# A hybrid recurrent and attention block: second norm written in place, row factors on VectorE, early matmuls that only occupy TensorE, one weight group finished feature by feature, and the modulation blocks laid out anew

## The chip, the cores and the metric

The kernel runs on one core of a Trainium2 chip. A core has a matrix engine (TensorE; PE in the profile, with PEld for its weight loads), a vector engine (VectorE; DVE), an engine for activation functions (ScalarE; ACT), a general engine (GpSimd; POOL) and a queue processor that issues most transfers (SyncE; SP). The metric is the device time of one execution in microseconds; lower is better.

## The reference

One layer on x of shape (512, 2048) in float32. A conditioning vector c gives six modulation vectors of 2048 values:

```
mod = silu(c) @ w_ada + b_ada
sh1, sc1, gt1, sh2, sc2, gt2 = split(mod, 6)
h = rms_norm(x, g_mix) * (1 + sc1) + sh1
xr, yr, q, k, v, f_logit = split(h @ w_in)
y_rec = scan(conv(xr), gates) * gelu(yr)          # 1024 features, 8 blocks of 128
y_att = softmax(norm(q) norm(k)^T + cum - cum^T, causal) v   # 8 heads of 128
mix = concat(rms_norm(y_rec, g_out_rec), rms_norm(y_att, g_out_att))
x = x + gt1 * (mix @ w_out)
h2 = rms_norm(x, g_ffn) * (1 + sc2) + sh2
gate, up = split(h2 @ w_up)                       # 5632 features each
x = x + gt2 * ((silu(gate) * up) @ w_down)
```

cum is the running sum over the tokens of log sigmoid(f_logit + b_f), one per head.

## The kernel before, in words

All large products are made in a split form: an operand is rounded to the fast float32 form (`hi`), what is left over is kept (`lo`), and hi·hi, hi·lo and lo·hi are added in PSUM. So each weight tile needs one ScalarE copy and one VectorE subtraction (`wsplit`, L220 to L225), and each pair of tiles three matmuls (`mm`, L228). Features lie on the 128 partitions and the 512 tokens along the row for most stages. A "k-tile" is 128 rows of the contraction; there are 16.

The stages in order, by the names that their PSUM tiles have in the profile:

- `cps`: the second half of c is spread over the partitions by two matmuls with one row each, and SiLU follows (L108 to L112). Then VectorE has silu(c) in all partitions, and each modulation value is a multiply-and-sum of a row of w_ada with it: one "ada block" is 128 such values, two instructions of 128x1024 (L148, or L158 in the early, unqueued form `ada_fast`).
- `w1p`: xr, 8 features' tiles over 16 k-tiles (L358 to L384). Each k-tile needs an ada block for sc1, the factor `A`, the split `hph`, `hpl` of x·A, and the split of the weights. The sum of squares `ssq_x` runs along.
- `rstd_x`: the row factor 1/rms of each token. `rstd_parts` (L281) has two halves: `sums` adds the squares over partitions with four tiny matmuls and calls `rms_rstd` (L273: mean plus eps, then a power of -0.5, all on GpSimd), and `spread` brings the four columns back to all partitions with four matmuls against the identity. For x both halves are called at once by `rstd_bcast` (L396).
- `yr0p`: the first four tiles of yr (`fm_group`, L420). At fixed k-tiles hooks call `sh1_block`: an ada block for sh1 and `make_h` (L401), which makes the normalised h of one k-tile out of x, `rstd_x` and sh1. Six more such blocks hang on the next group.
- `h0p` to `h7p`: q, k, v of one head each, tokens on partitions (`tm_group`, L259). While one group's matmuls run, the attention of the head before it and, from head 2 on, the recurrent blocks in pairs run from hooks at given k-tiles (ATT_STEPS, REC_STEPS). `forget` (L447) makes cum in two hooks, at steps 4 and 6 of the first group after head 0; `make_spn` (L604) makes softplus of the recurrent parameter, which depends on inputs only. In `attention`, `qk_t` transposes q and k and also makes the bias tiles `bt`; `score` adds them, takes the exponential and multiplies by the reciprocal of the row's sum (L555), `pt_` transposes, `pv` multiplies with v.
- `yr1p`: the other four tiles of yr, then GeLU and the product with the scan's output (L814 to L826).
- `wo0p` to `wo3p`: the output projection in four groups; the eight attention tiles come first in the contraction. `mix_sums` and `mix_rec` (L831, L835) hang on steps 1 and 4 of the first group; `mix_rec` makes the spread of both row factors and splits the eight recurrent tiles.
- `up0p`, `up1p`, then `uf4p` to `uf43p` with seven products in place of eight, then the down projection `dn4p` to `dn2p`. The operands T of the seven products are made by `make_t` (L973) out of `make_h2` (L961), at hooks of up0 and up1.

48 ada blocks (gt1, sh2, sc2) wait in a list. `ada1` takes one block from it, behind the last weight split that has been traced, and starts the load of the next; five or six hooks per group do this from head 2 on, and WO_ADA=5 per output group. What is left in the list when the last output group ends is done by `with_a2` (L851) ahead of the factor `a2`, with which `make_hr` (L858) makes the operands of up0.

The order of the instructions on each engine is made by a planner ahead of the run: it takes what is ready by its own estimate of durations, the earlier traced or higher in priority first (`high_priority` moves an instruction up), and `issue_after` puts an instruction behind a given one on its engine. Each engine then works strictly in that order. Tiles with one tag share a number of buffers; a load waits until its buffer is free. The tag `ada` has two buffers, which one block fills, the tag `whi` and `wlo` three each, and the PSUM tag `acc` four.

Of the kernel before, what the change touches and what calls it, by code (L numbers as in the profile page):

```python
# [66 lines left out]
def block_kernel(ctx, tc, xT, crow, adaT, vecs, bfr, w1, wyr, wqkv0, wqkv, wgate, wout, wup0, wups, wdn, outT):  # L67
# [33 lines left out]
    with tc.high_priority(offset=100000):  # L101
        cr = wp.tile([P, 2048], F32, tag="raw", name="cr", bufs=RAW)
        nc.sync.dma_start(out=cr[:1, 1024:2048], in_=crow[:, 1024:2048])
        nc.sync.dma_start(out=c_b[:, :1024], in_=crow[:, :1024].broadcast_to([P, 1024]))
        one = cp.tile([P, P], F32, name="ones")
        nc.vector.memset(one, 1.0)
        nc.scalar.activation(c_b[:, :1024], c_b[:, :1024], AF.Silu)
        for q in (2, 3):  # L108
# [2 lines left out]
            nc.tensor.matmul(pc, lhsT=one[:1, :], rhs=cr[:1, cs], start=True, stop=True)
# [161 lines left out]
    def rms_rstd(ssum, out, n, inv=None):  # L273
        nc.gpsimd.tensor_scalar(out=out, in0=ssum, scalar1=1.0 / n, scalar2=EPS, op0=ALU.mult, op1=ALU.add)
# [2 lines left out]
        nc.gpsimd.tensor_tensor(out, out, mhalf[:, :out.shape[-1]], ALU.pow)
        if inv is not None:
            nc.gpsimd.tensor_mul(inv, inv, out)

    def rstd_parts(ssq, n, name, inv=None, times=None, bank=None):  # L281
# [4 lines left out]
        def sums():  # L286
            if len(ssq.shape) == 3:
                nc.vector.tensor_reduce(out=tok, in_=ssq, axis=AX.X, op=ALU.add)
            else:
# [3 lines left out]
                nc.vector.tensor_copy(out=tok, in_=ps[:, :NT])  # L293
            rms_rstd(tok, tok, n, inv)
            if times is not None:
                nc.gpsimd.tensor_mul(tok, tok, times)
# [1032 lines left out]
```

## Time and profile before

| | |
|---|---|
| three runs | 2059.55, 2063.02, 2065.53 us; median 2063.02 |
| the profiled execution | 2058.99 us, of which the span of the trace is 2057.3 us |
| busy: PE, DVE, ACT, POOL | 2028.0, 1706.8, 945.7, 110.6 us |
| instructions | 32497 |
| mean granted clock of TensorE | 0.998 |

The page gives for each engine the busy time in the span. A line of a timeline is: start in us, duration in us, engine, line of the kernel, operation, output and inputs, shapes, how many were merged, and in brackets the idle time before it with what ended it. A line of the waits is: who waited, for whom, then total us, times, longest us. The recorded duration of one matmul is longer than its share, since matmuls overlap; the distance from start to start is its price.

### The profile page before, as it was taken

To read this page: it belongs to the slowest core of one execution; us is meant where nothing else is said; L and a number is where in the kernel's file an instruction comes from. 1 tells how busy PE (TensorE), PEld (TensorE's weight loads), DVE (VectorE), ACT (ScalarE), POOL (GpSimd) and SP (SyncE) were. 2 spreads that over 40 slices of the span, in tenths; PEclk is the share of its full clock that TensorE was granted. 3 is DMA by queue.
4 is the path that set the end of the run, shared out by engine and by line. 5 is a ranking of instruction groups with operands and counts; after the bars stand their busy time and mean duration, and the time that the engine had idled before them with its cause. 6 is when DMAs were issued, how large, how long until landed. Compare 5 with 4: busy or idle time off the path is not lost.

```text
span 2057.3 us, 32497 instructions
## 1 busy us (share of the span) xinstructions
PE 2028.0 (99%) x12505; PEld 1847.4 (90%) x12505; DVE 1706.8 (83%) x2549; ACT 945.7 (46%) x1321; POOL 110.6 (5%) x141
## 2 busy tenths in 40 slices
PE   8999999999999999999999999999999999999999
PEld 6889998888788888999999999999999978888887
DVE  8999769987887649988898889888898877777796
ACT  4433447765422446444444444444444444545443
POOL 0000111111100000001000000000000000000000
PEclk9999999999999999999999999999999999999999
DMA  9989866767778732348888879988888586676894
GB/s 345 339 287 319 283 216 220 237 210 247 253 273 314 271 133 100 123 136 226 255 232 230 244 226 256 263 235 228 240 240 224 167 279 240 238 250 240 280 327 167
DMA packets 175822, 493.36 MB, mean 240 GB/s; under 512 B 20625, under 2 KB 45105, under 8 KB 171570
## 3 DMA queue, kind: packets, MB, share of 16 engines
q1 hardware_dynamic: 156306, 437.79, 62.2%
q0 software_dynamic: 10144, 36.70, 9.4%
q10 hardware_dynamic: 9216, 16.78, 2.3%
q8 instruction: 98, 1.61, 0.3%
q14 instruction: 58, 0.48, 0.1%
HBM read 455.53 MB, written 93.35 MB: 267 GB/s over the span
## 4 chain that ended last, share of the span: by engine, by line
PE 89%; DVE 7%; DMA 2%; issue 1%; POOL 1%; ACT 0%; SPq 0%; DVEq 0%; POOLq 0%; ACTq 0%
PE w1p L228 4%; PE dn6p L228 3%; PE dn3p L228 3%; PE dn2p L228 3%; PE dn7p L228 3%; PE dn1p L228 3%; PE dn5p L228 3%; PE dn4p L228 2%; PE yr1p L228 2%; PE up0p L228 2%; PE wo2p L228 2%; PE wo3p L228 2%; PE wo1p L228 2%; PE up1p L228 2%; PE yr0p L228 2%; PE wo0p L228 2%
## 5 line engine op out<-in xcount | busy, mean ns | idle before, releaser
L148 DVE SCALAR_TENSOR_TENSOR ada<-ada,c_b 128x1024 f32<-128x1024 f32 x96 | 116.2, 1220 | 24.1 <-DMA ada<-in_adaT 24.0
L223 ACT ACTIVATE uq_0sh<-uq_0r 128x1024 fp32r<-128x1024 f32 x40 | 42.4, 1060 | 113.5 <-DVE uq_0r L1081 110.4
L224 DVE TENSOR_TENSOR uq_0tl<-uq_0r,uq_0th 128x1024 fp32r<-128x1024 f32 x40 | 49.0, 1225 | 37.4 <-ACT uq_0th L223 37.4
L223 ACT ACTIVATE uq_0ah<-uq_0r 128x1024 fp32r<-128x1024 f32 x40 | 42.4, 1060 | 69.1 <-PE uf39p L1103 1.8
L1020 POOL DMA_DIRECT2D s2d<-in_wdn x44 | 36.4, 828 | 673.8 <-DMA s2d<-in_wdn 660.4
L223 ACT ACTIVATE uq_1ah<-uq_1r 128x1024 fp32r<-128x1024 f32 x40 | 42.4, 1061 | 59.3 <-issue 26.6
L224 DVE TENSOR_TENSOR uq_0al<-uq_0r,uq_0ah 128x1024 fp32r<-128x1024 f32 x40 | 49.0, 1226 | 24.9 <-ACT uq_0ah L223 23.6
L224 DVE TENSOR_TENSOR uq_0sl<-uq_0r,uq_0sh 128x1024 fp32r<-128x1024 f32 x40 | 49.0, 1226 | 18.3 <-ACT uq_0sh L223 18.3
L1123 ACT ACTIVATE ug<-ug 128x512 f32<-128x512 f32 x40 | 25.3, 632 | 84.3 <-DVE ug L1120 84.3
L223 ACT ACTIVATE uq_0th<-uq_0r 128x1024 fp32r<-128x1024 f32 x40 | 42.4, 1060 | 43.9 <-PE uf6p L1103 1.2
L223 ACT ACTIVATE uq_1th<-uq_1r 128x1024 fp32r<-128x1024 f32 x40 | 42.4, 1061 | 32.8 <-PE uf43p L1103 1.1
L223 ACT ACTIVATE uq_1sh<-uq_1r 128x1024 fp32r<-128x1024 f32 x40 | 42.5, 1062 | 27.7 <-DVE uq_1r L1081 26.2
L228 PE MATMUL w1p<-hph,w1h 128*128 128x512 f32 x128 | 47.2, 399 | 5.7 <-ACT hph L370 5.7
L224 DVE TENSOR_TENSOR uq_1tl<-uq_1r,uq_1th 128x1024 fp32r<-128x1024 f32 x40 | 48.9, 1222 | 4.3 <-ACT uq_1th L223 3.2
L228 PE MATMUL w1p<-hpl,w1h 128*128 128x512 f32 x128 | 50.9, 398 | 0.1
L228 PE MATMUL w1p<-hph,w1l 128*128 128x512 f32 x128 | 50.8, 397 | 0.0
L224 DVE TENSOR_TENSOR uq_1sl<-uq_1r,uq_1sh 128x1024 fp32r<-128x1024 f32 x40 | 49.0, 1225 | 0.0
L1080 DVE TENSOR_TENSOR uq_0r<-uq_0r 128x1024 f32<-128x1024 f32 x40 | 48.8, 1219 | 0.0
L224 DVE TENSOR_TENSOR uq_1al<-uq_1r,uq_1ah 128x1024 fp32r<-128x1024 f32 x40 | 48.7, 1218 | 0.0
L1080 DVE TENSOR_TENSOR uq_1r<-uq_1r 128x1024 f32<-128x1024 f32 x40 | 48.7, 1217 | 0.0
L178 DVE SCALAR_TENSOR_TENSOR gt<-gt,c_b 128x512 f32<-128x512 f32 x64 | 43.8, 684 | 0.0
L158 DVE SCALAR_TENSOR_TENSOR ada<-ada,c_b 128x1024 f32<-128x1024 f32 x32 | 38.9, 1217 | 2.1 <-DMA ada<-in_adaT 2.1
(12769 smaller groups left out, 8123.2 us busy)
## 6 DMA issues: line engine op xcount, KB each, us to landing
ada<-in_adaT SPq DMA_DIRECT2D x128, 512.0 KB, 5.2
uq_1r<-in_wups SPq DMA_DIRECT2D x80, 512.0 KB, 8.0
uq_0r<-in_wups SPq DMA_DIRECT2D x80, 512.0 KB, 5.1
s2d<-in_wdn POOLq DMA_DIRECT2D x44, 512.0 KB, 9.0
adf<-in_adaT SPq DMA_DIRECT2D x32, 512.0 KB, 5.9
gt<-in_adaT ACTq DMA_DIRECT2D x64, 256.0 KB, 5.6
s2d<-in_wdn SPq DMA_DIRECT2D x22, 512.0 KB, 8.4
s4d<-in_wdn SPq DMA_DIRECT2D x22, 512.0 KB, 9.5
```

The lines of the kernel that those rows point to most:

```text
L148: nc.vector.scalar_tensor_tensor(out=t, in0=t, scalar=1.0, in1=cs, op0=ALU.mult, op1=ALU.mult, accum_out=ac)
L158: nc.vector.scalar_tensor_tensor(out=t, in0=t, scalar=1.0, in1=c_b[:, cs], op0=ALU.mult, op1=ALU.mult, accum_out=ada_acc[j][:, hf, i:i + 1])
L178: nc.vector.scalar_tensor_tensor(out=t, in0=t, scalar=1.0, in1=c_b[:, r * S:(r + 1) * S], op0=ALU.mult, op1=ALU.mult, accum_out=gt2_acc[:, ...
L223: tail_hi.append(nc.scalar.activation(R(hi[:, :n]), raw_ap, AF.Copy).ins)
L224: tail_lo.append(nc.vector.tensor_sub(R(lo[:, :n]), raw_ap, hi[:, :n]).ins)
L228: nc.tensor.matmul(ps, lhsT=R(l), rhs=R(r), start=start, stop=stop)
L1020: nc.gpsimd.dma_start(out=out[:, cs], in_=src[:, cs], accum_op=ALU.add)
L1080: nc.vector.tensor_add(blocks[:, 0:3:2], blocks[:, 0:2], blocks[:, 2:3].broadcast_to([P, 2, 512]))
L1123: nc.scalar.activation(g, g, AF.Silu)
```

## The change

- **Second norm in place.** `make_h2` writes into the tile `x1[kt]` itself. Before, it took one of two buffers.
- **Row factors.** In `rms_rstd` the mean plus eps and the products with the inverse move from GpSimd to VectorE, with raised priority; only the power stays on GpSimd. The mean is read from PSUM where it lies there. `rstd_bcast` goes; the spread of `rstd_x` becomes a hook of the first yr group at step 1, and the first two `sh1_block` hooks come at step 1.
- **The beginning.** The load of `vec` moves from SP's queue to ScalarE's, and `keep_on` adds matmuls whose result nobody reads: two of 128 columns ahead of the `cps` matmuls, eight behind them, and two of 512 columns with the first x tile. `make_spn` is put behind a weight split (`late=True`).
- **Forget sums.** `rest` is cut in two; three hooks at steps 1, 6 and 9. The bias tiles of `qk_t` become a step of their own, and head 0 gets its own list of steps.
- **Second yr group.** The last four k-tiles are taken feature by feature, and each feature's GeLU and product follow at once.
- **Output groups.** The ada hooks are at (11, 14), (0, 4, 8, 12), (0, 3, 6, 9, 12), (0, 3, 6, 9) in place of (0, 3, 6, 9, 12) in each. The spread for the attention's factor stays at step 4, the rest of `mix_rec` moves to step 5.

```diff
-FORGET_STEP = 4
+FORGET_STEPS = (1, 6, 9)
+RX_STEP = 1
-WO_ADA = 5
+WO_ADA = ((11, 14), (0, 4, 8, 12), (0, 3, 6, 9, 12), (0, 3, 6, 9))
+KEEP = (2, 8, 2)
...
+        nc.scalar.dma_start(out=vec, in_=vecs)
         one = cp.tile([P, P], F32, name="ones")
...
+        keep = acc("keep")
+        def keep_on(n, rhs):
+            for _ in range(n):
+                nc.tensor.matmul(keep[:, :rhs.shape[-1]], lhsT=one, rhs=rhs, start=True, stop=True)
+        keep_on(KEEP[0], one)
         for q in (2, 3):
...
-        nc.sync.dma_start(out=vec, in_=vecs)
+        with tc.issue_after(last.ins):
+            keep_on(KEEP[1], one)
...
+        held = []
         for n, (kt, hi, lo) in enumerate(stream(src, kts, width, name, **kw)):
+            if n >= len(kts) - by_feature:
+                held.append((n, kt, hi, lo))
+                continue
             for f in range(nf):
+                cell(n, f, kt, hi, lo)
...
+        for f in range(nf if held else 0):
+            for n, *w in held:
+                cell(n, f, *w)
+            if evac:
+                evac(f, ps[f])
+            for fn in hooks.get(held[f][0], ()) if hooks else ():
+                fn()
...
     def rms_rstd(ssum, out, n, inv=None):
-        nc.gpsimd.tensor_scalar(out=out, in0=ssum, scalar1=1.0 / n, scalar2=EPS, op0=ALU.mult, op1=ALU.add)
-        if inv is not None:
-            nc.gpsimd.tensor_copy(out=inv, in_=out)
-        nc.gpsimd.tensor_tensor(out, out, mhalf[:, :out.shape[-1]], ALU.pow)
-        if inv is not None:
-            nc.gpsimd.tensor_mul(inv, inv, out)
+        with tc.high_priority(offset=EVAC):
+            mean = out if inv is None else inv
+            nc.vector.tensor_scalar(out=mean, in0=ssum, scalar1=1.0 / n, scalar2=EPS, op0=ALU.mult, op1=ALU.add)
+            nc.gpsimd.tensor_tensor(out, mean, mhalf[:, :out.shape[-1]], ALU.pow)
+            if inv is not None:
+                nc.vector.tensor_mul(inv, inv, out)
...
+                if kt == 0:
+                    keep_on(KEEP[2], xt)
...
-    rstd_x = rstd_bcast(ssq_x, D, "rstd_x", bank=acc)
+    rx_sums, rx_spread = rstd_parts(ssq_x, D, "rstd_x", bank=acc)
+    rx_sums()
...
-    hk0 = {}
+    hk0 = {RX_STEP: [lambda: rx.append(rx_spread())]}
     for kt in range(10):
-        hk0.setdefault(kt * 8 // 5, []).append(lambda kt=kt: sh1_block(kt))
+        hk0.setdefault(max(RX_STEP, kt * 8 // 5), []).append(lambda kt=kt: sh1_block(kt))
...
-        log1p_exp(spn, zl, NB, "spn")
+        log1p_exp(spn, zl, NB, "spn", late=True)
...
-    yr1 = fm_group(wyr[1], list(range(KT)), hs_, "yr1", hooks=hk)
+    yr1 = fm_group(wyr[1], list(range(KT)), hs_, "yr1", hooks=hk, by_feature=4,
+                   evac=lambda f, p: rec_out(4 + f, gelu2(p, f"ge{4 + f}", "c")))
...
-        for n in range(WO_ADA):
-            add(hk, 16 * n // WO_ADA, ada1)
+        for n in WO_ADA[g]:
+            add(hk, n, ada1)
         if g == 0:
             add(hk, MIXREC_STEPS[0], mix_sums)
-            add(hk, MIXREC_STEPS[1], mix_rec)
+            add(hk, MIXREC_STEPS[1], lambda: st_att.append(att_spread()))
+            add(hk, MIXREC_STEPS[1] + 1, mix_rec)
...
-        t = ap_.tile([P, S], F32, tag="x", name=f"h2x{kt}", bufs=2)
-        nc.vector.scalar_tensor_tensor(out=t, in0=x1[kt], scalar=a2[:, kt:kt + 1], in1=r1[0], op0=ALU.mult, op1=ALU.mult)
+        t = x1[kt]
+        nc.vector.scalar_tensor_tensor(out=t, in0=t, scalar=a2[:, kt:kt + 1], in1=r1[0], op0=ALU.mult, op1=ALU.mult)
```

More of the change, by code (lines that the diff above doesn't have):

```diff
@@ L110, in block_kernel @@
             pc = acc(f"cps{q}")
-            nc.tensor.matmul(pc, lhsT=one[:1, :], rhs=cr[:1, cs], start=True, stop=True)
+            last = nc.tensor.matmul(pc, lhsT=one[:1, :], rhs=cr[:1, cs], start=True, stop=True)
             nc.scalar.activation(c_b[:, cs], pc, AF.Silu)
-        nc.sync.dma_start(out=vec, in_=vecs)
+        with tc.issue_after(last.ins):
+            keep_on(KEEP[1], one)
     ident = cp.tile([P, P], F32, name="ident")
@@ L292, in sums @@
                     nc.tensor.matmul(ps[:, t:t + 1], lhsT=ssq[:, t * P:(t + 1) * P], rhs=ones[:, 0:1], start=True, stop=True)
-                nc.vector.tensor_copy(out=tok, in_=ps[:, :NT])
-            rms_rstd(tok, tok, n, inv)
+            rms_rstd(tok if len(ssq.shape) == 3 else ps[:, :NT], tok, n, inv)
             if times is not None:
-                nc.gpsimd.tensor_mul(tok, tok, times)
+                with tc.high_priority(offset=EVAC):
+                    nc.vector.tensor_mul(tok, tok, times)
         def spread():
@@ L306, in rstd_parts @@
         return sums, spread
-    def rstd_bcast(*a, **kw):
-        sums, spread = rstd_parts(*a, **kw)
-        sums()
-        return spread()
     def square_acc(ssq, src, first, name, tag):
@@ L324, in log1p_exp @@
         q = small(w, name + "q", 2)
-        nc.scalar.activation(e, z, AF.Abs)
+        if late:
+            with tc.issue_after(tail_hi[-1]):
+                nc.scalar.activation(e, z, AF.Abs)
+        else:
+            nc.scalar.activation(e, z, AF.Abs)
         nc.scalar.activation(e, e, AF.Exp, scale=-1.0)
@@ L406, in make_h @@
         t = xs[kt]
-        nc.vector.scalar_tensor_tensor(out=t, in0=t, scalar=A[kt], in1=rstd_x, op0=ALU.mult, op1=ALU.mult)
+        nc.vector.scalar_tensor_tensor(out=t, in0=t, scalar=A[kt], in1=rx[0], op0=ALU.mult, op1=ALU.mult)
         h, l = page(f"hh{kt}", "h"), page(f"hl{kt}", "h")
@@ L523, in qk_t, with biases @@
             st["qk"] = qkT
+        def biases():
             if h == 0:
@@ L813, in block_kernel @@
         add(hk, MIX_STEPS[i], lambda i=i: mix_att(i))
-    yr1 = fm_group(wyr[1], list(range(KT)), hs_, "yr1", hooks=hk)
+    yr1 = fm_group(wyr[1], list(range(KT)), hs_, "yr1", hooks=hk, by_feature=4,
+                   evac=lambda f, p: rec_out(4 + f, gelu2(p, f"ge{4 + f}", "c")))
     for i in range(4, NH):
         mix_att(i)
-    gy = []
-    for f in range(4):
-        g, w = yr1[f], page(f"ge{4 + f}", "c")
-        nc.scalar.activation(w, yr1[f], AF.Square)
-        nc.vector.scalar_tensor_tensor(out=w, in0=w, scalar=1.0 / GELU_C, in1=g, op0=ALU.add, op1=ALU.mult)
-        nc.scalar.activation(w, w, AF.Tanh, scale=GELU_C * GELU_S)
-        nc.vector.scalar_tensor_tensor(out=w, in0=w, scalar=1.0, in1=g, op0=ALU.add, op1=ALU.mult)
-        gy.append(w)
-    for f in range(4):
-        rec_out(4 + f, gy[f])
     st_att = []
```

38 lines of the change are left out of this document (22 added, 16 removed).

## The prediction

> **What bounds the kernel now.** I read the busy shares first, then the list of what TensorE waited for, then the timelines around each of these waits. The page:
>
> ```profile
> span 2057.3 us, 32497 instructions
> PE 2028.0 (99%) x12505; PEld 1847.4 (90%) x12505; DVE 1706.8 (83%) x2549; ACT 945.7 (46%) x1321; POOL 110.6 (5%) x141
> ```
>
> TensorE idles for 2057.3 - 2028.0 = 29.3 us, so no change that leaves the matmuls alone can win much more than that. The waits of TensorE (total us, times, longest):
>
> ```profile
> PE pt L561 <- DVE bt L555: 6.7, 5, 2.3
> PE w1p L228 <- ACT hph L370: 5.7, 1, 5.7
> PE uf4p L1103 <- ACT uq_0ch L1077: 1.9, 1, 1.9
> PE rstd_xb L301 <- POOL rstd_xt L277: 1.8, 1, 1.8
> PE ratiob L301 <- POOL ratiot L296: 1.5, 1, 1.5
> PE pc L460 <- DVE lf L458: 1.4, 1, 1.4
> PE h0p L228 <- ACT hh L409: 0.9, 1, 0.9
> PE wo0p L228 <- ACT mx3h L216: 0.8, 1, 0.8
> ```
>
> Nearly every one of these lines is touched by the change. Each is a gap of a serial engine, so a closed gap moves all that follows, unless VectorE is full there and becomes the bound. That is the question at each step.
>
> **The beginning.** TensorE's timeline, the start and the first matmuls; then the price of a warm matmul from a long unbroken stretch of the chain; then the first matmul after w1p:
>
> ```profile
> 2.44 3.75 PE L111 MATMUL cps<-cr,ones 1*128 1x512 f32 x4 [2.44 <-DMA cr<-in_crow]
> 11.87 1.22 PE L228 MATMUL w1p<-hph,w1h 128*128 128x512 f32 x2 [5.69 <-ACT hph L370]
> 17.61 0.58 PE L228 MATMUL w1p<-hph,w1h 128*128 128x512 f32 x1
> 18.04 0.39 PE L228 MATMUL w1p<-hpl,w1h 128*128 128x512 f32 x1
> 1873.05 60.01 PE dn6p L228 x264
> 102.15 0.39 PE L228 MATMUL yr0p<-hph,yr_0h 128*128 128x512 f32 x1
> ```
>
> Up to 17.61 a matmul takes 0.43 us from start to start (18.04 - 17.61), and from there on 60.01/264 = 0.2273, as its shorter records (0.39 for 0.58) show too: the clock is at half until then. The second k-tile began at 102.15 - 15 x 24 x 0.2273 = 20.3. VectorE's timeline has the operands (`hpl` of the first, second and last k-tile) and one of the softplus instructions among them, and ScalarE's shows when x arrives:
>
> ```profile
> 12.30 0.16 DVE L333 SCALAR_TENSOR_TENSOR spn<-spn,spnq 128x8 f32<-128x8 f32 x1
> 12.38 0.74 DVE L371 SCALAR_TENSOR_TENSOR hpl<-x,A,hph 128x512 fp32r<-128x512 f32 x1
> 18.09 0.75 DVE L371 SCALAR_TENSOR_TENSOR hpl<-x,A,hph 128x512 fp32r<-128x512 f32 x1
> 94.11 0.74 DVE L371 SCALAR_TENSOR_TENSOR hpl<-x,A,hph 128x512 fp32r<-128x512 f32 x1
> 9.95 0.63 ACT L315 ACTIVATE ssq_x<-x 128x512 f32<-128x512 f32 x1 [1.34 <-DMA x<-in_xT]
> ```
>
> The second matmul waits for the first `hpl`, done at 13.1. The softplus chain (13 VectorE instructions of about 0.16, several of them between `A` and `hpl`) leaves this place, and `vec` leaves SP's queue ahead of the first ada load: I take 0.6 us for both, `hpl` at 12.5. If the clock is full by then, the k-tile ends at 12.5 + 23 x 0.2273 = 17.7 in place of 20.3: **-2.6**. VectorE permits it: the second `hpl` ends at 18.8, less about 1 us of softplus work, and the sixteenth at 94.9 against TensorE's need at 20.3 + 14 x 5.455 = 96.7 in the old timeline, about 2 us of room plus that 1 us. The cost of the added matmuls: two `cps` of 512 columns took 3.75, so one takes 1.9 and one of 128 columns 0.47. Eight of them fill 6.2 to 9.9 at the slow clock, with no real work ready. The two with x start at 9.95 and end at 11.9 warm or 13.7 cold; only the cold case delays anything, by 13.7 - 13.1 = 0.6. On ScalarE the issue of `vec` comes ahead of SiLU, which waits for c anyway; on VectorE the instructions that read `vec` stand ahead of the first ada block, so it must land before that one's load, as it did on SP's queue. Bounds: +0.6 to -2.9.
>
> The trace alone says only that 5.7 us of idling left the clock slow and that some 6 us of work raised it. [...]
>
> **The row factor of x, and a stretch where VectorE is full.** GpSimd's chain, VectorE's wait for it, VectorE's last operand for h0, and a window in between (busy of PE, PEld, DVE, ACT, POOL, then granted clock, DMA share, GB/s):
>
> ```profile
> 105.18 1.09 POOL L274 TENSOR_SCALAR rstd_xt<-rstd_xt 128x4 f32<-128x4 f32 x1 [103.55 <-DVE rstd_xt L293]
> 106.36 1.91 POOL L277 TENSOR_TENSOR rstd_xt<-rstd_xt,mhalf 128x4 f32<-128x4 f32 x1
> 110.15 0.75 DVE L407 SCALAR_TENSOR_TENSOR x<-x,A,rstd_x 128x512 f32<-128x512 f32 x1 [2.78 <-ACT rstd_x L304]
> 183.20 0.75 DVE L410 SCALAR_TENSOR_TENSOR hl<-x,sh,hh 128x512 fp32r<-128x512 f32 x1
> 140.00:160.00 20.00, 20.00 (x102) 18.33 (x101) 20.00 (x35) 6.17 (x8) 0.00 (x0) 1.00 0.99 337
> ```
>
> With the spread behind two k-tiles TensorE's wait of 1.8 goes: 24 matmuls (5.5) and the tiny sums after 102.15 put it at about 108.5, and the power, without the 1.09 ahead of it, is done near 107.2. But from 110 to 184 VectorE does not pause, and h0's last k-tile already waits 0.9 for it. On TensorE's side this stage could gain 2.6 + 1.8 + 0.9 = 5.3. On VectorE's side the chain starts again at the spread, which moves with the beginning (-2.6) and lies 0.2 later (108.5 against 108.3), plus what of the 2.78 idle the planner fills with ada blocks, now that it knows of a later spread. I take half, 1.4: -2.6 + 0.2 - 1.4 = **-3.8 for the beginning and this stage together**; bounds +0.8 and -5.3.
>
> **Forget sums.** The chain `lf` now has five k-tiles before its matmul (each 12 matmuls of 384 columns, 12 x 0.75 x 0.2273 = 2.0 us): **-1.4**, bounds 0 and -1.4. The 13 softplus instructions come into this place; VectorE fills it with bias sums that wait for nobody.
>
> **Row factors in the heads.** Head 3's factor, and the window behind it:
>
> ```profile
> 314.78 1.10 POOL L274 TENSOR_SCALAR ss<-ss 128x8 f32<-128x8 f32 x1 [25.23 <-DVE ss L504]
> 315.96 1.64 POOL L277 TENSOR_TENSOR ss<-ss,mhalf 128x8 f32<-128x8 f32 x1
> 317.63 0.69 DVE L511 TENSOR_TENSOR qk<-qk,ss 128x512 f32<-128x512 f32 x1 [1.80 <-POOL ss L277]
> 362.78 0.69 DVE L511 TENSOR_TENSOR qk<-qk,ss 128x512 f32<-128x512 f32 x1 [0.30 <-POOL ss L277]
> 409.07 0.69 DVE L511 TENSOR_TENSOR qk<-qk,ss 128x512 f32<-128x512 f32 x1 [1.80 <-POOL ss L277]
> 320.00:340.00 20.00, 20.00 (x115) 19.17 (x115) 20.00 (x39) 18.22 (x30) 2.68 (x4) 1.00 0.55 196
> ```
>
> In the heads with recurrent pairs VectorE is full from here to the late `bt`, so its wait for GpSimd reaches TensorE. 1.1 of the chain goes and one VectorE instruction of about 0.2 comes (as the 0.16 above): -0.9 in heads 3 and 5, -0.3 in head 4, where it waited only 0.30, and about half of 0.9 in the last head, whose `bt` is the last of the five waits: **-2.5**. Bounds 0 (the planner spends it on other work) and -6.7 (all five waits).
>
> **End of the second yr group.** The wait for `ratio` and the next one behind it are 1.5 + 0.8. GeLU began when the whole group was done:
>
> ```profile
> 542.04 1.87 DVE L821 SCALAR_TENSOR_TENSOR ge<-ge,yr1p 128x512 f32<-128x512 f32 x3
> 567.45 1.42 DVE L840 SCALAR_TENSOR_TENSOR hsr<-hsr,vec,ratio 128x512 f32<-128x512 f32 x2 [1.93 <-ACT ratio L304]
> ```
>
> By features the first PSUM tile is complete 36 matmuls, 8.2 us, sooner, the last at the old time; four chains that queued at 542 are spread over 534 to 548, and three ada blocks (2 x 1.22 each) leave the first output group. **-2.3**, bounds 0 and -2.3. The new product with the inverse on VectorE waits there for the power (1.9); behind it stand splits of wo0, each due in 5.5 us at the earliest, so I price it at 0. What the feature order can cost: two weight buffers of three are held to the end, so the next group's second split starts about 1.4 us before that end, and it is needed 5.5 us after it.
>
> **Ada blocks.** The new list holds 2 + 4 + 5 + 4 = 15 hooks. 31 blocks go into the heads and yr1, of 48: **two are left for `with_a2`**, ahead of `a2`. VectorE and TensorE:
>
> ```profile
> 693.71 2.08 DVE L862 SCALAR_TENSOR_TENSOR hrl<-x,a,hrh 128x512 fp32r<-128x512 f32 x3 [0.79 <-ACT hrh L861]
> 712.23 1.23 DVE L224 TENSOR_TENSOR wo_1l<-wo3r,wo_1h 128x1024 fp32r<-128x1024 f32 x1 [2.30 <-ACT wo_1h L223]
> 727.41 1.43 DVE L944 SCALAR_TENSOR_TENSOR x<-wo3p,mod,rstd_att 128x512 f32<-128x512 f32 x2 [3.08 <-PE wo3p L228]
> 729.25 0.39 PE L228 MATMUL up0p<-hrh,up_0h 128*128 128x512 f32 x1
> DMA to landing us min/median/max: 3.0/5.9/8.6
> ```
>
> `hrl` is traced behind the evacuation of L944 but ran 34 us ahead of it: the planner pulls forward what is ready. So the two blocks run right behind the last split of wo3: 713.5 to 715.9 the first; its buffers free the second load, 5.9 more, 721.8 to 724.2 the second, `a2` at 724.8, the first operands (0.7 + 0.75) at 726.3. TensorE asks at 729.25. **0**, with 3.0 us of slack; the slowest landing leaves 0.3. The operand work of about 8 us moves from 693 to 718 into the up0 group, whose k-tiles take 2.7 each.
>
> **Second norm in place.** uf4's wait of 1.9 is for the split `uq_0ch`, which stands on ScalarE's queue behind the last `h2x`:
>
> ```profile
> 823.82 0.72 ACT L964 ACTIVATE h2x<-h2x,mod 128x512 f32<-128x512 f32 x1 [1.59 <-DVE h2x L963]
> ```
>
> That `h2x` needed one of two buffers, held by the tile before it; in place it can be made earlier, and ScalarE's idle 1.59 goes: **-1.5**, bounds 0 and -1.9.
>
> **Sum.** -3.8 - 1.4 - 2.5 - 2.3 + 0 - 1.5 = -11.5. The profiled execution took 2058.99 (1.7 around its span), 4.0 below the median of 2063.02; so 2047.5 on its scale, and 2051.5 on that of the median.
>
> **The rivals.**
> - *VectorE swallows the first half.* The clock stays slow (-0.6 of the beginning remains, the spread's gap is given back at h0), and the heads' order spends the 2.5 elsewhere: -0.6 - 1.4 - 2.3 - 1.5 = -5.8, 2057.2. For it: the full windows above. Against: the 2.78 of idle.
> - *Everything closes.* -5.3 - 1.4 - 6.7 - 2.3 - 1.9 = -17.6, 2045.4. Against it: VectorE's full windows.
> - *Late `a2`, slower.* The planner puts the two blocks behind the evacuation at 727.4: 730 to 732.3, load 5.9, second block to 740.5, `a2` 741, operands 742.5. up0 starts 13 us late, and cold again (13 x 0.2 = 2.6): +15.6, 2067.1. It decides once `a2` is later than 727.8, and turns the sign past 740. Against it: the 34 us above.
> - *It does not do what it says.* The planner reorders everything and opens as many waits as it closes: 2063.
>
> **Chances.** Forecast 0.50, its own range 2047 to 2055; swallowed 0.25; everything 0.10; late `a2` 0.08; nothing 0.07. The 0.3% that a measurement of this kernel can tell is 6.2 us, so faster means below 2056.8: 0.50 + 0.10 + half of the swallowed case 0.12 = 0.72. Slower than 2069.2 is the tail of the late `a2`: 0.04. Same: 0.24. The range 2045 to 2061 leaves out the late `a2`, nothing, and the tail of the best case.
>
> **What would show it.** Right: matmuls 0.23 apart from the first k-tile on; no wait at `rstd_xb`, `pc`, `ratiob`; h0's wait at most about 2; waits for `bt` summing to about 4; up0 without a gap. Wrong: 0.43 apart past 12 us, a longer wait at h0p, a wait of up0p for `hrh`, or new waits of yr1p for its splits.

## The result, and the profile after

The changed kernel takes **2050.88 us** (median of six runs, 2049.28 to 2053.46) beside 2062.65 for the kernel before (six runs, 2059.55 to 2065.53): ratio **0.9944, 95% interval 0.9931 to 0.9957**. The forecast was 2051.5. Its profiled execution took 2049.87. One of the ten executions of a kernel below (before, with the second norm in place) took 2853.05 us at a mean granted clock of 0.655 and is left out of its ratio.

The page of the changed kernel, and what its TensorE waited for (total us, times, longest):

```profile
span 2048.2 us, 32491 instructions
...
PE 2030.6 (99%) x12529; PEld 1850.5 (90%) x12529; DVE 1707.4 (83%) x2560; ACT 944.7 (46%) x1321; POOL 98.1 (5%) x126
```
```profile
PE pt L597 <- DVE bt L591: 7.9, 5, 2.6
PE h0p L239 <- ACT hh L437: 1.4, 1, 1.4
...
PE h1p L239 <- DVE z L480: 0.7, 1, 0.7
...
PE po L609 <- ACT pT L601: 0.5, 1, 0.5
...
```

The rows for `w1p`, `rstd_xb`, `pc`, `ratiob`, `wo0p` and `uf4p`, each 0.8 to 5.7 before, are gone. The largest row, `bt`, is not smaller but larger: 7.9 for 6.7. The list alone does not say what each wait was worth; the times at which each stage's first matmul starts do. Shift is after minus before, step is what the stage ahead of it gave. The starts are rounded to 0.1 us, so a step, and what is reckoned from it, can be 0.1 off. For uf4p and uf5p it is the first matmul with `tb0h`, the thirteenth of the group, since in the kernel before two of uf5p's first ones stand among the last of uf4p:

| first matmul of | before | after | shift | step | step as forecast |
|---|---|---|---|---|---|
| yr0p | 102.2 | 99.2 | -3.0 | -3.0 (beginning) | -2.6 |
| h1p | 185.5 | 181.4 | -4.1 | -1.1 (row factor of x, less what h0 gave back) | -1.2 |
| h2p | 228.3 | 223.0 | -5.3 | -1.2 (forget sums) | -1.4 |
| h5p | 355.8 | 351.7 | -4.1 | +1.2 (nearly all of it in the group h2p) | |
| h6p | 400.5 | 399.6 | -0.9 | +3.2 (head 4) | |
| wo0p | 542.7 | 540.5 | -2.2 | -1.3 (most of it head 5) | -2.5 for the three rows of heads together |
| wo1p | 593.4 | 588.3 | -5.1 | -2.9 (ratio) | -2.3 |
| up0p, uf4p | 729.3, 822.3 | 724.2, 817.2 | -5.1 | 0 (ada blocks, a2) | 0 |
| uf5p | 846.6 | 837.4 | -9.2 | -4.1 (second norm) | -1.5 |

Behind uf5p nothing moves. Two steps are far from the forecast: the heads lose 3.1 where 2.5 were to be won, and the second norm in place brings 4.1 for 1.5.

The beginning in TensorE's timeline of the changed kernel:

```profile
2.27 3.78 PE L121 MATMUL cps<-cr,ones 1*128 1x512 f32 x4
5.98 3.78 PE L115 MATMUL keep<-ones 128*128 128x128 f32 x16
9.91 2.12 PE L115 MATMUL keep<-x,ones 128*128 128x512 f32 x4
11.82 1.19 PE L239 MATMUL w1p<-hph,w1h 128*128 128x512 f32 x4
12.86 0.39 PE L239 MATMUL w1p<-hpl,w1h 128*128 128x512 f32 x1
13.08 0.39 PE L239 MATMUL w1p<-hph,w1l 128*128 128x512 f32 x1
17.49 1.19 PE L239 MATMUL w1p<-hph,w1h 128*128 128x512 f32 x4
```

The eight added matmuls of 128 columns run slowly (0.47 each) up to 9.8. The two with x take 1.06 each, where a `cps` of the same width takes 1.89: the clock rises during the first of them (the first of the four records is 0.84 long, the others 0.59). From 12.86 on a matmul takes 0.22 to 0.23, and the second k-tile begins at 17.5 in place of 20.3.

For the second norm, these rows give the first matmuls with `tb0h` of two successive groups (name, count, durations in ns, first and last start). The kernel before comes first, with its wait behind these rows, then the kernel after:

```profile
L1103 PE MATMUL uf4p<-tb0h,uq_0ah x2: 283/283/283, 822.3 to 822.6; 128*128 128x256 f32 x2
L1103 PE MATMUL uf5p<-tb0h,uq_0ah x2: 283/283/283, 846.6 to 847.0; 128*128 128x256 f32 x2
...
825.78 0.39 PE L1103 MATMUL uf4p<-tc0h,uq_0ch 128*128 128x256 f32 x1 [1.91 <-ACT uq_0ch L1077]
827.35 0.41 PE L1103 MATMUL uf4p<-tc2h,uq_0ch 128*128 128x256 f32 x1
827.57 0.41 PE L1103 MATMUL uf4p<-tc2l,uq_0ch 128*128 128x256 f32 x1
```
```profile
L1131 PE MATMUL uf4p<-tb0h,uq_0ah x2: 283/283/283, 817.2 to 817.6; 128*128 128x256 f32 x2
L1131 PE MATMUL uf5p<-tb0h,uq_0ah x2: 283/283/283, 837.4 to 837.8; 128*128 128x256 f32 x2
```

From uf4p to uf5p it is 20.2 us after and 24.3 before. Of the 4.1 the row of the wait shows only 1.9; 1.5 more lie **behind** it, where 16 matmuls up to 830.3 are 0.21 apart in place of 0.12: the clock had fallen to half. The rest are gaps of 0.1 to 0.2 us in the timeline from 839 on.

The heads, at head 4. First the kernel before (GpSimd's mean and power, and VectorE's ada block beside them), then the changed kernel (ada block, mean, power, product with the factor):

```profile
360.83 0.20 POOL L274 TENSOR_SCALAR ss<-ss 128x8 f32<-128x8 f32 x1 [22.01 <-DVE ss L504]
361.11 1.64 POOL L277 TENSOR_TENSOR ss<-ss,mhalf 128x8 f32<-128x8 f32 x1
361.25 1.22 DVE L148 SCALAR_TENSOR_TENSOR ada<-ada,c_b 128x1024 f32<-128x1024 f32 x1 [0.51 <-DMA ada<-in_adaT]
```
```profile
357.19 1.21 DVE L159 SCALAR_TENSOR_TENSOR ada<-ada,c_b 128x1024 f32<-128x1024 f32 x1
358.33 0.17 DVE L301 TENSOR_SCALAR ss<-ss 128x8 f32<-128x8 f32 x1
358.57 1.64 POOL L302 TENSOR_TENSOR ss<-ss,mhalf 128x8 f32<-128x8 f32 x1 [23.86 <-DVE ss L301]
360.25 0.69 DVE L545 TENSOR_TENSOR qk<-qk,ss 128x512 f32<-128x512 f32 x1 [1.75 <-POOL ss L302]
```

GpSimd's mean had cost 1.10 in head 3 (in the prediction's rows) and costs 0.20 here, where the ada block came late from its transfer. After, the block stands between the reduction and the mean, and VectorE then idles for the whole power. From the reduction's start to the product it is 4.21 in heads 3, 5, 6 and 7 before and 4.25 after; in head 4 it is 3.31 before and 4.25 after.

### The profile page after: what moved, and what is told of

It reads as the page before. It is cut to its first block, busy times and chain, and to the rows that moved or that the text cites. A ratio compares the mean times of both kernels' runs of the same rounds, so it can differ in the third digit from the quotient of the medians.

```text
span 2048.2 us, 32491 instructions
## 1 busy us (share of the span) xinstructions
PE 2030.6 (99%) x12529; PEld 1850.5 (90%) x12529; DVE 1707.4 (83%) x2560; ACT 944.7 (46%) x1321; POOL 98.1 (5%) x126
## 4 chain that ended last, share of the span: by engine, by line
PE 90%; DVE 4%; issue 2%; DMA 2%; SPq 0%; ACT 0%; POOL 0%; DVEq 0%; ACTq 0%; POOLq 0%
PE w1p L239 4%; PE dn6p L239 3%; PE dn3p L239 3%; PE dn2p L239 3%; PE dn7p L239 3%; PE dn1p L239 3%; PE dn5p L239 3%; PE dn4p L239 2%; PE yr1p L239 2%; PE up0p L239 2%; PE yr0p L239 2%; PE wo2p L239 2%; PE wo3p L239 2%; PE wo1p L239 2%; PE up1p L239 2%
## 5 line engine op out<-in xcount | busy, mean ns | idle before, releaser
L239 PE MATMUL w1p<-hph,w1h 128*128 128x512 f32 x128 | 42.4, 391 | 0.0
```

The costliest lines, as they stand in the source:

```text
L239: nc.tensor.matmul(ps, lhsT=R(l), rhs=R(r), start=start, stop=stop)
```

## The experiments

Medians and ratios are against the kernel before, run on the same chip in turn with them; differences in stages come from the profiles.

| kernel | median us | ratio (95% interval) |
|---|---|---|
| the changed kernel, again | 2051.03 | 0.9948 (0.9932 to 0.9964) |
| heads' mean on GpSimd | 2053.52 | 0.9954 (0.9942 to 0.9967) |
| block right behind the mean | 2057.25 | 0.9981 (0.9971 to 0.9990) |
| block 0.4 us behind the mean | 2053.62 | 0.9957 (0.9942 to 0.9971) |
| without added matmuls | 2055.22 | 0.9966 (0.9956 to 0.9977) |
| second norm in a buffer | 2057.79 | 0.9976 (0.9965 to 0.9987) |
| before, second norm in place | 2058.69 | 0.9985 (0.9975 to 0.9995) |
| yr1 all together | 2055.93 | 0.9967 (0.9956 to 0.9979) |
| four blocks left | 2061.51 | 1.0003 (0.9990 to 1.0017) |
| head 0 on the common steps | 2049.20 | 0.9937 (0.9919 to 0.9954) |
| two blocks out of heads 3 to 5 | 2049.32 | 0.9933 (0.9920 to 0.9946) |
| one block out of heads 3 to 5 | 2044.18 | 0.9912 (0.9897 to 0.9926) |

**The same kernel again.**

> The kernel after, unchanged, beside the others on this chip: 2051. Its profile tells how far stage lengths differ between two executions of one program. If the order of instructions alone sets them, every stage is within 0.5 us of the first profile; if transfers set some, the heads' groups differ by 1 to 3 us, at waits that end with a transfer.

Stage starts agree within 0.3 us up to h2p and within 1.0 behind it. Two groups differ by more than the 0.5 that the first theory allowed: h3p takes 1.6 longer and h6p 1.4 less, and not at a wait for a transfer. The waits for `bt` in heads 3, 4 and 5 are 2.30, 2.61, 2.02 (2.30, 2.63, 1.87 in the first profile). So the order of instructions sets the waits, and what differs is mainly the clock: it is at half for 3.41 us from 270.6 and from 390.1 here, from 389.1 and from 436.9 in the first profile. From the down projection's first to its second phase this profile has 0.8 more. A single profile tells the start of a stage to about 1 us, and the length of one group to about 1.7.

**The added matmuls taken out.**

```diff
-KEEP = (2, 8, 2)
+KEEP = (0, 0, 0)
```

> The kernel after, without the twelve matmuls whose result nobody reads (the counts 2, 8, 2 set to zero); vec on ScalarE's queue and the late softplus stay. Theory: the clock of w1p's first k-tile is again at half, 0.43 us from matmul to matmul up to about 17.5 us: yr0p starts 2 us later than in the kernel after (99.2), and what VectorE gives back at h0p is less than half, so the time is 2052 to 2053. Rival (VectorE sets the pace through the first half and swallows it): yr0p 2 us later, h0p where it is, 2050.5 to 2051.5.

TensorE's timeline of this kernel:

```profile
12.06 0.79 PE L239 MATMUL w1p<-hph,w1h 128*128 128x512 f32 x1 [5.96 <-ACT hph L396]
...
13.87 0.63 PE L239 MATMUL w1p<-hph,w1h 128*128 128x512 f32 x1
14.29 0.63 PE L239 MATMUL w1p<-hpl,w1h 128*128 128x512 f32 x1
```

The matmuls are 0.42 apart again, up to 16.8. yr0p starts at 101.6 (+2.4), h0p and h1p 2.4 later too: all of it goes through VectorE's full stretch, and the rival that VectorE swallows it is wrong. So 2.4 of the beginning's 3.0 are the added matmuls. The other 0.6, as much as I had put on `vec` and the late softplus, is a remainder: no run takes these two out. The median lies 4.3 above the changed kernel's, more than either theory gave. A further 2.4 of the profile arise between h3p and h7p, where nothing was edited: three groups are 1.6 to 1.9 longer and one is 2.7 shorter. The stretches at half clock lie elsewhere, from 272.8, 347.9 and 440.1, three in place of two.

**The second norm, undone in the kernel after and done alone in the kernel before.**

```diff
-        t = x1[kt]
-        nc.vector.scalar_tensor_tensor(out=t, in0=t, scalar=a2[:, kt:kt + 1], ...)
+        t = ap_.tile([P, S], F32, tag="x", name=f"h2x{kt}", bufs=2)
+        nc.vector.scalar_tensor_tensor(out=t, in0=x1[kt], scalar=a2[:, kt:kt + 1], ...)
```

> The kernel after, with the second norm written into one of two buffers again, as in the kernel before. Theory: the wait of uf4p (1.9 us) is back, and TensorE runs at half clock for some 3.4 us behind it (matmuls of 256 columns 0.21 apart in place of 0.12), so uf4p takes 24 us again and the time is 2054 to 2055.5. Rival (the wait alone, as forecast; the other 2 us of this stage come from another part): 2052 to 2053.

> The kernel before with the second norm written in place, and nothing else of the change. Theory: this alone takes the wait of uf4p and the half clock behind it: uf4p to uf5p 20.2 us in place of 24.3, and the time 2058.5, 4.1 below the kernel before. Rival (the wait alone, as forecast): 1.5 to 1.9 below, 2061.

Undone, the wait of 1.9 is back, 16 slow matmuls behind it, and uf4p takes 24.4 again (+4.2 against the changed kernel). The median, 6.9 above the changed kernel's, lies above both ranges: in the profile 2.5 arise ahead of the edited stage and 1.2 in the down projection. Done alone in the kernel before (its rows):

```profile
L1103 PE MATMUL uf4p<-tb0h,uq_0ah x2: 283/283/283, 821.3 to 821.7; 128*128 128x256 f32 x2
L1103 PE MATMUL uf5p<-tb0h,uq_0ah x2: 283/283/283, 841.5 to 841.8; 128*128 128x256 f32 x2
```

Here it is 20.2, so -4.1 in this stage; the medians differ by 3.6. In this stage the one line of the change is worth about 4, needed and sufficient.

**The end of yr1 taken together again.**

```diff
-    yr1 = fm_group(wyr[1], list(range(KT)), hs_, "yr1", hooks=hk, by_feature=4, evac=...)
+    yr1 = fm_group(wyr[1], list(range(KT)), hs_, "yr1", hooks=hk)
+    for f in range(4):
+        rec_out(4 + f, gelu2(yr1[f], f"ge{4 + f}", "c"))
```

> The kernel after, with all 16 k-tiles of the second yr group taken together again; GeLU and the product follow for each feature when the whole group is done. Theory: TensorE waits for the ratio's spread again, about 1.5 us and 0.8 behind it, so from wo0p to wo1p it is 2.3 to 3 us longer than the kernel after's 47.8, and the time is 2053 to 2054. Rival (the gain of this stage came from the row factors on VectorE and from the ada blocks that left the first output group): wo0p to wo1p within 0.5 us of 47.8, 2051.

```profile
PE wo0p L239 <- ACT mx0h L227: 1.5, 1, 1.5
```

From wo0p to wo1p it is 51.0 for 47.8, +3.2. The wait's place is not the one I named: the ratio itself is early enough, the first recurrent tile `mx0h` is late, one step further down the same chain, and `mx0l` and `mx2l` behind it cost 0.5 and 0.4 more. The median, 2055.93, lies above both ranges. Of the 6.0 by which this profile lies behind the changed kernel's, 2.1 arise in the heads, ahead of the edit, with three stretches at half clock for two, and 0.9 in the down projection.

**More ada blocks left for the end.**

```diff
-WO_ADA = (..., (0, 3, 6, 9))
+WO_ADA = (..., (0, 5))
```

> The kernel after, with two ada blocks fewer in the last output group, so that four instead of two are left for the factor a2. Theory (the reckoning of the prediction's rival, with this kernel's rows): the blocks follow the last split of wo3 (708.3) one behind the other, 8 us each, since each waits for its buffers and its load: 708, 716, 724, 732, a2 at about 736.5, first operands at 738.5; up0p starts 14 us late, its first matmuls partly at half clock: 2065 to 2068. Rival (the planner finds another place for them, the blocks' loads come closer together): below 2058.

VectorE's row of the factor `a2`, in the changed kernel and here:

```profile
720.20 0.17 DVE L882 SCALAR_TENSOR_TENSOR a<-mod,vec 128x16 f32<-128x16 f32 x1
```
```profile
736.66 0.17 DVE L882 SCALAR_TENSOR_TENSOR a<-mod,vec 128x16 f32<-128x16 f32 x1
```

I had expected 736.5. up0p starts 13.4 later; 2.2 of this come back by up1p, and the median lies 10.6 above the changed kernel's, below the range of the theory (2065 to 2068) and above the rival's. So the mechanism of the slower rival is real; with two blocks left it does not reach TensorE.

**The heads: mean on GpSimd, block behind the mean, block 0.4 us behind it.**

```diff
+        if n == HEAD_DIM:
+            nc.gpsimd.tensor_scalar(out=out, in0=ssum, scalar1=1.0 / n, scalar2=EPS, ...)
+            nc.gpsimd.tensor_tensor(out, out, mhalf[:, :out.shape[-1]], ALU.pow)
+            return
```

> The kernel after, with the mean of the heads' row factors back on GpSimd (only for the eight heads; the three other factors keep it on VectorE). Theory: moving the mean bought nothing in the heads, because the planner's filler, an ada block of 1.2 us that used to lie beside GpSimd's mean, now stands on VectorE between the reduction and the mean, so VectorE still waits 1.75 us for the power. Undone, the stretch from h5p to h6p loses its extra 3.2 us (wait for bt 2.6 back to 1.4 and no half clock behind it), head 5's gain of 1.4 is lost: net 2048 to 2052, where the kernel after has 2050.9. Rival (the mean on VectorE is worth the forecast 2.5, and the 3.2 us come from elsewhere, the order of the bias tiles or of the steps): 2053 to 2054, and h5p to h6p as long as in the kernel after (47.9 us from first matmul to first matmul).

Head 4 of this kernel, VectorE and GpSimd:

```profile
362.56 1.21 DVE L159 SCALAR_TENSOR_TENSOR ada<-ada,c_b 128x1024 f32<-128x1024 f32 x1
362.73 1.10 POOL L300 TENSOR_SCALAR ss<-ss 128x8 f32<-128x8 f32 x1 [22.72 <-DVE ss L542]
363.91 1.64 POOL L301 TENSOR_TENSOR ss<-ss,mhalf 128x8 f32<-128x8 f32 x1
365.58 0.69 DVE L549 TENSOR_TENSOR qk<-qk,ss 128x512 f32<-128x512 f32 x1 [1.80 <-POOL ss L301]
```

The median is in the rival's range, but not for the rival's reason: from h3p to h7p this profile has 184.4 us for the changed kernel's 182.6, and the largest difference, 4.0 from h1p to h2p, is head 0's wait for `bt` (3.1 for 0.7) and 3.41 us at half clock behind it. VectorE's wait for a transfer of the bias sums there is 1.95 for 0.70. In heads 3 to 7 half of my theory stands: the mean's place is worth nothing, VectorE waits 1.80 for 1.75. The other half falls: with the mean on GpSimd head 4 does not get back the short wait of the kernel before (2.62 for `bt`). That one came from the block's late transfer, not from the mean. And in heads 2 to 7 the mean on GpSimd takes 1.10 whenever the block begins 0.2 us ahead of it, 0.20 when it does not: the 0.9 is a wait for VectorE, no work (in the rows above the mean ends at 363.83, the block's instruction at 363.77).

```diff
+    def ada_behind():
+        with tc.issue_after(means[-1]):
+            ada_some(1)
...
+            m = nc.vector.tensor_scalar(out=mean, in0=ssum, scalar1=1.0 / n, scalar2=EPS, op0=ALU.mult, op1=ALU.add)
+            if n == HEAD_DIM:
+                means.append(m.ins)
...
             for n in H_ADA:
-                add(hk, n, ada1)
+                add(hk, n, ada_behind if n == 4 else ada1)
```

> The kernel after, with the ada block of each group's fourth k-tile put behind the mean of the head's row factor on VectorE, so that the mean comes 1.2 us sooner and the block runs beside GpSimd's power. Nothing else is moved. Theory: VectorE's wait for the power falls from 1.75 to about 0.6 in heads 2 to 6, each wait for bt falls by up to 1.2 us (2.30, 2.63, 1.87 to 1.1, 1.4, 0.7), and the half clock behind the longest goes: 2044 to 2048. Rival (VectorE is full up to the last bt, and what the wait loses is only filled by other work that was due later anyway): 2050 to 2051.5.

Head 3 here, where the mean is at 310.87:

```profile
310.95 1.22 DVE L159 SCALAR_TENSOR_TENSOR ada<-ada,c_b 128x1024 f32<-128x1024 f32 x1
311.12 2.54 POOL L308 TENSOR_TENSOR ss<-ss,mhalf 128x8 f32<-128x8 f32 x1 [23.45 <-DVE ss L305]
313.69 1.29 DVE L551 TENSOR_TENSOR qk<-qk,ss 128x512 f32<-128x512 f32 x2 [1.52 <-POOL ss L308]
```

Neither range holds. In heads 3, 5, 6 and 7 the power takes 2.54 beside the block, the wait only goes from 1.75 to 1.52, and the kernel is slower by 6.4; the profile puts the loss into h3p to h7p (188.1 us for 182.6), at waits for `bt` of 2.5 and 0.8 + 2.0 and a new one of 1.7 for the copies of head 5's PSUM. Head 4 is different: there the block waits for its transfer and begins 0.65 behind the power, the power takes 1.64, the product starts 3.37 after the reduction, and the wait for `bt` is only 0.9.

```diff
+            if n == HEAD_DIM and pending:
+                with tc.issue_after(m.ins):
+                    m = nc.vector.tensor_reduce(out=idle, in_=c_b[:, :256], axis=AX.X, op=ALU.add)
+                means.append(m.ins)
...
+              with (tc.issue_after(filler[-1]) if h >= 2 else ExitStack()):
                 nc.vector.tensor_tensor(z, z, ss[:, 4 * a:4 * a + 4].unsqueeze(2).broadcast_to([P, NT, P]), ALU.mult)
...
-                add(hk, n, ada1)
+                add(hk, 2 if n == 4 else n, ada_behind if n == 4 else ada1)
```

> The kernel after; in heads 2 to 7 the mean of the row factor is followed on VectorE by a small reduction with one input (128x256, its result unused), then by the ada block that stood ahead of the mean, and the product with the factor comes behind that block. Theory from the runs so far: the power takes 1.64 us by itself and 2.54 when an ada block (two inputs from SBUF) begins on VectorE within 0.2 us of it, so a filler right behind the mean wins nothing; 0.4 us later it does not disturb the power. Then VectorE no longer idles 1.75 us in these heads, the waits for bt in heads 3, 4 and 5 fall from 2.3, 2.6 and 1.9 by 1.2 to 1.6 each, and the time falls to 2045 to 2048. Rival (the power is slowed by any work of VectorE beside it, or the product is now late by as much): power 2.5 or longer, and the time 2050 to 2057, as with the block right behind the mean.

Head 3: the power, the block, and VectorE 10 us later:

```profile
312.35 1.64 POOL L316 TENSOR_TENSOR ss<-ss,mhalf 128x8 f32<-128x8 f32 x1 [23.45 <-DVE ss L311]
312.50 1.22 DVE L161 SCALAR_TENSOR_TENSOR ada<-ada,c_b 128x1024 f32<-128x1024 f32 x1
...
321.08 1.22 DVE L161 SCALAR_TENSOR_TENSOR ada<-ada,c_b 128x1024 f32<-128x1024 f32 x1 [1.78 <-DMA ada<-in_adaT]
```

A block that begins 0.15 behind the power disturbs it no more, and is not held by it: the rival's reason is wrong, its range right. VectorE's idle at the power is closed, and the time does not fall: 1.78 idle appear where the next block waits for its transfer, and the waits for `bt` are 3.3, 1.3 and 0.9 + 2.0. The product, put behind the block, starts 4.60 after the reduction for 4.25, so this run closes VectorE's wait without shortening the chain. It shows that the idle time alone was not worth its price: in heads 3 and 5 the waits for `bt` grow, only in head 4 the wait falls, from 2.63 to 1.27.

**What does keep bt late: the blocks.** In the changed kernel, the end of head 4's chain, on VectorE, ScalarE and TensorE:

```profile
385.23 0.68 DVE L587 CUSTOM_DVE_ANT_0 bt<-s,bt 128x512 f32<-128x512 f32 x1
385.95 0.72 ACT L589 ACTIVATE bt<-bt,nm 128x512 f32<-128x512 f32 x1 [0.31 <-DVE nm L587]
386.44 1.21 DVE L159 SCALAR_TENSOR_TENSOR ada<-ada,c_b 128x1024 f32<-128x1024 f32 x1
387.59 0.15 DVE L590 RECIPROCAL sm<-sm 128x1 f32<-128x1 f32 x1
388.25 0.48 DVE L591 TENSOR_SCALAR bt<-bt,sm 128x512 f32<-128x512 f32 x1
388.78 0.85 PE L597 MATMUL pt<-ident,bt 128*128 128x128 f32 x4 [2.63 <-DVE bt L591]
```

The exponential and its row sum are done at 386.8, and the reciprocal stands behind an ada block of 1.2.

```diff
-            for n in H_ADA:
+            for n in (1, 4, 7) if 3 <= h < 6 else (1, 3, 6, 8, 11, 13) if h >= 6 else H_ADA:
-WO_ADA = ((11, 14), (0, 4, 8, 12), (0, 3, 6, 9, 12), (0, 3, 6, 9))
+WO_ADA = ((6, 8, 10, 12, 14), (0, 4, 8, 12), (0, 3, 6, 9, 12), (0, 3, 6, 9, 12))
```

> The kernel after, with two of the five ada blocks (those of k-tiles 10 and 13) taken out of the groups behind heads 3, 4 and 5 and laid into the two groups behind heads 6 and 7 (six blocks each), the first output group (five) and the last (five); two are still left for the end. Theory: the waits for bt in heads 3, 4 and 5 (2.3, 2.6 and 2.0 us, and 1.7 to 2 us of half clock behind one or two of them) are VectorE's backlog of ada blocks, 1.2 us each, between the mean and the last bt; three or four of them less there (after: 5 or 6 instructions, now 2) leave only the chain score, reduction, exponential, product: waits below 0.7 each, the time 2043 to 2047. Rival (the waits are that chain itself, since the planner's order leaves two k-tiles between the last score and the transposes): waits as long as before, the time 2050 to 2052, or more where the first output group waits for its ratio.

Heads 4 and 5 have no wait for `bt` left, head 3 one of 1.85; h7p starts 6.2 sooner than in the changed kernel. Then it is given back: 3.8 up to wo0p, 1.3 at wo0p, 1.3 at up0p. The median, 2049.32, lies in neither range. The largest loss, VectorE and TensorE at the start of yr1p:

```profile
487.74 1.23 DVE L159 SCALAR_TENSOR_TENSOR ada<-ada,c_b 128x1024 f32<-128x1024 f32 x1 [1.81 <-DMA ada<-in_adaT]
...
488.89 0.42 DVE L524 COPY qk<-h7p 128x256 f32<-128x256 f32 x1
...
489.68 0.50 PE L239 MATMUL yr1p<-hh,yr_0h 128*128 128x512 f32 x1 [1.73 <-ACT v L527]
```

A moved block waits 1.81 for its transfer, in order ahead of a copy that empties h7p's PSUM; ScalarE's copies wait for VectorE's (up to 2.7), TensorE for ScalarE's (1.73).

**Head 0's own list of steps.**

```diff
-        for n, f in zip((FIRST_STEPS if h == 0 else ATT_STEPS if h < NH - 1 else LAST_STEPS)[1:], att[1:]):
+        for n, f in zip((ATT_STEPS if h < NH - 1 else LAST_STEPS)[1:], att[1:]):
```

> The kernel after, with head 0 on the same list of steps as the other heads (its own list had been put in by the change). Theory: the waits of 0.7 for bt and 0.5 for pT in head 0's group come from the later steps of its own list; with the common one they go or shrink by about 1 us, but the bias tiles' place comes ahead of the running sums' transpose and TensorE may wait for cum there: 2050 to 2052, not to be told from no change. Rival (the own list is what keeps the forget sums off the path): a wait of 1 us or more for cum or bt in that group, 2052 to 2054.

The small waits in this group go, h3p starts 1.3 and 0.7 sooner than in the two profiles of the changed kernel. The medians are 2049.20 and 2051.03 and their intervals overlap, so the two are not told apart.

**One block out of heads 3 to 5.**

```diff
-            for n in H_ADA:
+            for n in (1, 4, 7, 10) if 3 <= h < 6 else (1, 4, 6, 8, 10, 13) if h == 2 else H_ADA:
...
-        for n, f in zip((FIRST_STEPS if h == 0 else ATT_STEPS if h < NH - 1 else LAST_STEPS)[1:], att[1:]):
+        for n, f in zip((ATT_STEPS if h < NH - 1 else LAST_STEPS)[1:], att[1:]):
...
-WO_ADA = ((11, 14), (0, 4, 8, 12), (0, 3, 6, 9, 12), (0, 3, 6, 9))
+WO_ADA = ((8, 11, 14), (0, 3, 6, 9, 12), (0, 3, 6, 9, 12), (0, 3, 6, 9))
```

> The kernel after, with head 0 on the common list of steps, and one ada block (that of k-tile 13) taken out of the groups behind heads 3, 4 and 5; one goes into the group behind head 2 (six blocks), where VectorE idles 3.6 to 6.8 us, one into the first output group (8, 11, 14), one into the second (0, 3, 6, 9, 12); the groups behind heads 6 and 7 and the last output group stay as in the kernel after, since there the moved blocks stood ahead of the evacuation of h7p and gave back 2.9 us, and 1.3 each at wo0p and up0p. Theory (blocks on VectorE set the waits for bt): h4p to h7p 2 to 4 us shorter than the kernel after's 140.2, nothing given back behind it, 1 us for head 0: 2045 to 2048. Rival (each block costs the same wherever it is put): 2049 to 2051.

```profile
span 2042.8 us, 32502 instructions
...
PE pt L597 <- DVE bt L591: 3.6, 4, 2.1
```

h4p to h7p takes 134.8 for 140.2, one stretch at half clock for two, nothing is given back ahead of the down projection, and the time is **2044.18, ratio 0.9912 (0.9897 to 0.9926)** to the kernel before: below the changed kernel's interval, and a little below the expected range. This interval overlaps that of head 0's list alone, whose edit this run contains; that edit lies ahead of h4p. VectorE still waits 1.63 to 1.75 for the power in heads 3 to 7. So with that wait left as it is, fewer blocks make `bt` come sooner.

## Why the prediction was right, and where it was not

The total was right, and two of its terms were not.

- **Beginning and row factor of x**, -3.8: measured -4.1. The split holds too (2.4 clock for 2.0, 0.6 the rest), and the added float32 matmuls do raise the clock, between 9.9 and 10.6. That it would be full by 12.5 was an assumption of mine that no run showed ahead of the change; with the added matmuls those of w1p are 0.22 to 0.23 apart from 12.86 on, without them 0.42 up to 16.8. No run undoes the row factor of x alone. h0 took back 0.9 of the 5.0 that had been won at h0p (waits of 1.4 and 0.7 there, 0.9 and 0.2 before).
- **Forget sums**, -1.4: measured -1.2, as a stage only; no run undoes them alone.
- **Row factors in the heads**, -2.5: measured +3.1 from h2p to wo0p. This is the step that failed, in two places. First, I read GpSimd's 1.10 as the price of a mean. The timeline of the kernel before had a row of 0.20 for head 4; the 1.10 are 0.20 of work and 0.9 of waiting for the ada block on VectorE (in head 3 that instruction ends at 315.82, the mean at 315.88). Moved, the block stands ahead of the mean instead, and the chain is as long as before (4.25 for 4.21). Second, I reckoned that VectorE's wait reaches TensorE through `bt` in every head. Closing that wait by the 0.4 us spacer did not shorten the waits for `bt` in heads 3 and 5; taking blocks away did. In head 4 the chain does count: where it is 3.3 to 3.4 long (the kernel before, also with the norm in place, and the block right behind the mean) the wait for `bt` is 0.9 to 1.4, and in the changed kernel, where it is 4.25, it is 2.6. The bound of 0 that I gave for "the planner spends it on other work" was the right reading, and a loss was not in the bounds. The loss itself is head 4: the kernel before had a late transfer there that let mean and power run ahead of the block, 0.94 of chain, and the wait for `bt` grew from 1.39 to 2.63, with half clock behind it.
- **Second yr group**, -2.3: measured -2.9, and 3.2 when undone.
- **Ada blocks**, 0: measured 0. `a2` was reckoned at 724.8 on the old scale; 720.2 plus the shift of 5.1 is 725.3.
- **Second norm**, -1.5: measured -4.1. The mechanism was right, its size was not: the bound of -1.9 counted the wait alone and left out the half clock behind it, which the rows of the kernel before showed.
- **Sum.** -11.5 forecast; by the profiles -9.1: 5.6 short in the heads, 2.6 more at the second norm, 0.6 more at the ratio and small ones. The medians differ by 11.8. Between the two profiled executions and the medians 2.7 are left, since the first lay 3.7 below its median and the second 1.0. That the forecast of 2051.5 came this near is in part the cancelling of these.

The medians of several kernels differ by some 2 us more than their edited stage. The granted clock on record accounts for much of it. A stretch of 3.41 us at half clock costs about 1.7, half of its length (h3p takes 43.9 with one and 42.3 without), and the profiles have different numbers of them in the heads: two in both profiles of the changed kernel, three without the added matmuls and with yr1 together, four with the heads' mean on GpSimd, one with one block out. The time of one kernel moves with its mean granted clock too: with the heads' mean on GpSimd an execution took 2048.65 us at 0.999 and another 2058.59 at 0.995. At 0.998 its three took 2050.82 to 2053.41 and the changed kernel's five 2049.28 to 2052.82, so its higher median is no price of the mean. What stays open is where the stretches lay in the executions that were not profiled.

## What to carry to other kernels

Where an engine's small instruction has two durations in one profile, ask what the other engine did at its start: here the difference (0.20 and 1.10) was a wait and not a price, and moving the instruction did not win it. Price a wait of TensorE with the matmuls behind it, start to start, since the clock may be at half there: behind uf4p's wait of 1.9 that cost 1.5 more. Before paying for a shorter chain ahead of a full engine, take filler off that engine; it was worth 5.4 us in the heads here, and put in the wrong place it came back as a wait for its own transfer, with other work in order behind it.
